# Two transformer blocks: an FFN's down projection over 512 tokens, and a PLE stage in a written order

## The chip, the cores and the metric

The kernel runs on one core of one Trainium2 chip. A core has TensorE (PE, matrix products), VectorE (DVE), ScalarE (ACT), GpSimd (POOL) and SyncE (SP), which issues the transfers. The metric is the device time of one execution in microseconds, as a median over runs. A profile of one execution gives the trace.

## The reference, cut to what matters

A first block of two layers gives h, 512 tokens by 1024 features. The second block has two layers, and each ends with these lines (`rms_norm(h, g)` is h / sqrt(mean(h²) + eps) · g, the mean over a token's features):

```python
h = h + rms_norm(mix, post_mix_g[i])
f = conv_ffn(rms_norm(h, pre_ffn_g[i]), w_up[i], conv_w[i], conv_b[i], w_down[i])   # (silu(g) * up) @ w_down
h = h + rms_norm(f, post_ffn_g[i])
gate = jax.nn.sigmoid(rms_norm(h, ple_norm_g[i]) @ w_ple_gate[i])
h = h + gate * (p[i] @ w_ple_proj[i])
```

`conv_ffn` has 2816 hidden features, its down projection goes from 2816 to 1024. The last two lines are the PLE: a projection of p (256 features) to 1024, times a gate of 1024 by 1024. Behind layer 0's PLE comes layer 1's mixer, which begins with `rms_norm(h, pre_mix_g)`; layer 1's PLE writes the output.

## The kernel before

Activations lie with features on the 128 partitions and tokens along the free dimension: h is 128 x 8 x 512. Every product is computed as three products of split float32 numbers. A weight tile w of 128 x 1024 is loaded by SP (`wload`, line 235), ScalarE rounds it to `whi` (L246) and another engine subtracts to get `wlo` (L249, `wsplit`). `lomode` says which: VectorE ("V"), or POOL and VectorE in turn ("VP", in the PLE's gate). Operands are split in the same way. `mm3_steps` then issues for each of the feature blocks three matmuls into one PSUM bank (L279).

The down projection stands at the end of `ffn_main`. `HALVES` are tokens 0 to 255 and 256 to 511. For each half and each of 8 blocks of output features, 22 hidden blocks are multiplied, with weights in three loads; all weights are loaded and split once for each half. `post_evac` copies a block to `fg` with the gain and adds its squares to `acc`. When half 0 is done, `post_add` turns its squares to a factor: TensorE sums over partitions with `mean1k` (`rsc`, L312), VectorE adds eps and POOL takes the power (`rcol`, L315 and L316), TensorE spreads the result over 128 partitions (`rsb`, L320). VectorE multiplies `fg` by it (L1108), POOL and VectorE in turn add it to h (L1109). `scaled_in` makes the gate's operand: ScalarE's copy (L1066) and VectorE's subtraction (L1067), `paA` for half 0 and `paB` for half 1. Half 0's steps run beside the matmuls of half 1.

The `ple` function does the same for half 1, then `scale` sums the squares of h for each half (L1073 ScalarE, L458 VectorE, L461 POOL) and gives `rr`, the norm's factor, which is applied after the product. 48 matmuls of 512 columns give the projection `pp` (L1665). The gate goes by `project8`: half 0 with all 8 weight blocks, then half 1 with the same weights, loaded and split again. For each block `gate` does four steps (L1670 to L1673). In layer 0 the next mixer's norm follows for each half (`norm_in`); the mixer loads its small constants and multiplies `ws` by a triangle mask `tri` (L1261).

An instruction's place in its engine's queue is set by a scheduler with its own model of durations, except inside `manual_schedule` for the engines it names: there they stand as the code issues them. Each engine runs its queue in order. Slots (`_Slots`) interleave generators of instructions: a main stream, whose items each carry a length in nanoseconds, and side streams, of which each takes one step for every call of the slot.

```python
# the slot: one step of every side stream, then the main stream for ns nanoseconds
self.sides = [x for x in self.sides if next(x, self) is not self]
self.debt += ns
```

## Time and profile before

| what | value |
|---|---|
| median of 3 runs | 2337.01 us (2332.03 to 2339.45) |
| the profiled execution | 2340.36 us, its span 2338.6 us |
| TensorE, VectorE, ScalarE, POOL busy | 2244.5, 1707.5, 1140.5, 510.6 us |
| layer 0: down projection from 1419.7, PLE from 1547.0 to 1613.5 us | 127.3 and 66.5 us |
| layer 1: down projection from 2142.1, PLE from 2269.3 to 2334.0 us | 127.2 and 64.7 us |
| mean granted clock of TensorE | 0.983 |

An engine's busy time is the sum of its instructions; the span is the time from the first instruction to the last. PE and PEld are TensorE's matmuls and its weight loads, which run beside each other. A granted clock of 1.00 is TensorE's upper level of 2.4 GHz, 0.50 the lower of 1.2 GHz. In the chain of waits a piece such as "x570" is a run of that many instructions without a gap, so its length divided by the count is the spacing from one start to the next.

### The profile page before, as it was taken

The numbers are of one execution on the slowest core, as the hardware profiler recorded it, in microseconds if no ns is written. First come the engines' busy times: TensorE is split into PE (matmuls) and PEld (weight loads), VectorE is DVE, ScalarE is ACT, GpSimd is POOL, SyncE is SP. The second block draws the span as 40 slices with busy tenths as digits, with TensorE's granted clock in tenths as the row PEclk, the third lists the DMA queues.
The fourth block names the chain that finished last, engine by engine and source line by source line (L and its number), as shares of the span: only waits on it lengthen the run. The fifth ranks groups of instructions, "written<-read, shape, count | busy, mean of one in ns | idle before, by whom it ended". The sixth has DMA issues, their size and how long they took to land.

```text
span 2338.6 us, 37220 instructions
## 1 busy us (share of the span) xinstructions
PE 2244.5 (96%) x14372; PEld 1948.9 (83%) x14372; DVE 1707.5 (73%) x2922; ACT 1140.5 (49%) x2105; POOL 510.6 (22%) x548
## 2 busy tenths in 40 slices
PE   7999999999999998998999999999998999999998
PEld 5877778888888897766898889988876798888998
DVE  5898656746888868877787665669878688666558
ACT  3534443643434344456664444555455665444444
POOL 0110010322444425113121110124204021110004
PEclk9999999999999998999999999999998999999999
DMA  7452124442122244420253335665430153334664
GB/s 287 127 162 92 37 86 148 145 125 90 56 64 64 75 147 148 162 64 28 78 175 99 99 97 148 178 185 178 144 116 19 54 164 118 99 99 116 174 189 136
DMA packets 83746, 279.03 MB, mean 119 GB/s; under 512 B 9584, under 2 KB 14704, under 8 KB 83568
## 3 DMA queue, kind: packets, MB, share of 16 engines
q1 hardware_dynamic: 83568, 276.64, 37.9%
q8 instruction: 113, 1.85, 0.3%
q14 instruction: 65, 0.53, 0.1%
HBM read 274.51 MB, written 2.10 MB: 118 GB/s over the span
## 4 chain that ended last, share of the span: by engine, by line
PE 76%; DVE 15%; ACT 3%; issue 3%; DMA 2%; POOL 2%; SPq 0%; DVEq 0%; ACTq 0%; POOLq 0%
PE mm L279 29%; PE bg L279 23%; PE s L279 4%; DVE wlo L249 3%; PE o L580 2%; PE s L924 2%; PE pt L571 2%; PE bg L845 2%; DMA w<-in_w_ada 2%; PE s L1564 1%; PE pt L279 1%; PE s L845 1%; PE bg L1665 1%; ACT whi L246 1%; PE mm L1377 1%
## 5 line engine op out<-in xcount | busy, mean ns | idle before, releaser
L246 ACT CAST whi<-w 128x1024 fp32r<-128x1024 f32 (+1 forms) x436 | 449.0, 1032 | 568.9 <-PE mm L279 250.2
L249 DVE TENSOR_TENSOR wlo<-w,whi 128x1024 fp32r<-128x1024 f32 (+1 forms) x420 | 524.0, 1250 | 225.1 <-ACT whi L246 222.8
L279 PE MATMUL bg<-a,whi 128*128 128x512 f32 x1280 | 395.7, 391 | 0.0
L279 PEld LDWEIGHTS bg<-a,whi 128*128 128x128 f32 x1280 | 240.4, 188 | 51.2 <-issue 1.0
L279 PE MATMUL mm<-hx,whi 128*128 128x512 f32 x864 | 276.7, 400 | 3.4 <-DVE sga L682 3.1
L279 PE MATMUL mm<-fh,whi 128*128 128x256 f32 x1408 | 252.7, 282 | 0.0
L279 PE MATMUL bg<-a,wlo 128*128 128x512 f32 x640 | 249.7, 391 | 2.6 <-DVE wlo L249 2.6
L279 PEld LDWEIGHTS mm<-fh,whi 128*128 128x128 f32 x1408 | 217.3, 189 | 0.2
L279 PE MATMUL mm<-fh,wlo 128*128 128x256 f32 x704 | 198.9, 284 | 0.6 <-DVE wlo L249 0.6
L279 PEld LDWEIGHTS mm<-hx,whi 128*128 128x128 f32 x864 | 158.4, 190 | 33.3 <-DVE sga L682 3.3
L279 PE MATMUL mm<-a,whi 128*128 128x256 f32 (+1 forms) x768 | 169.4, 316 | 2.4 <-DVE a L254 1.1
L279 PE MATMUL mm<-hx,wlo 128*128 128x512 f32 x432 | 170.1, 394 | 0.0
L1617 POOL TENSOR_TENSOR cv<-cv 128x512 f32<-128x512 f32 x44 | 61.6, 1400 | 386.1 <-DVE cv L1604 386.1
L279 PEld LDWEIGHTS bg<-a,wlo 128*128 128x128 f32 x640 | 120.6, 188 | 29.0 <-DVE wlo L249 4.0
L1604 DVE SCALAR_TENSOR_TENSOR cv<-q,cols,cv 128x511 f32<-128x511 f32 (+1 forms) x176 | 134.4, 766 | 2.5
L279 PEld LDWEIGHTS mm<-fh,wlo 128*128 128x128 f32 x704 | 132.5, 189 | 1.0 <-DVE wlo L249 1.0
L279 PEld LDWEIGHTS mm<-a,whi 128*128 128x128 f32 x768 | 124.8, 196 | 8.8 <-issue 2.3
L1611 DVE TENSOR_TENSOR q<-bg,rr 128x512 f32<-128x512 f32 x74 | 51.1, 691 | 107.6 <-PE bg L279 107.6
L279 PE MATMUL s<-a,whi 128*128 128x256 f32 (+1 forms) x576 | 116.4, 300 | 1.6 <-DVE a L254 1.6
L279 PE MATMUL mm<-a,wlo 128*128 128x256 f32 (+1 forms) x384 | 117.8, 307 | 0.0
L279 PE MATMUL mm<-hc,whi 128*128 128x256 f32 x576 | 110.0, 289 | 2.3 <-ACT k L813 2.2
L279 PEld LDWEIGHTS s<-a,whi 128*128 128x128 f32 x576 | 92.9, 194 | 5.6 <-DVE a L254 1.9
(461 smaller groups left out, 4948.9 us busy)
## 6 DMA issues: line engine op xcount, KB each, us to landing
w<-in_wup SPq DMA_DIRECT2D x102, 512.0 KB, 3.6
w<-in_wdn SPq DMA_DIRECT2D x64, 448.0 KB, 3.4
w<-in_w_ada SPq DMA_DIRECT2D x48, 512.0 KB, 3.6
w<-in_w_c SPq DMA_DIRECT2D x48, 512.0 KB, 3.5
w<-in_w_in SPq DMA_DIRECT2D x38, 512.0 KB, 4.5
w<-in_wo SPq DMA_DIRECT2D x32, 512.0 KB, 3.5
w<-in_wdn SPq DMA_DIRECT2D x32, 512.0 KB, 3.6
w<-in_wpg SPq DMA_DIRECT2D x32, 512.0 KB, 3.8
```

The costliest lines, as they stand in the source:

```text
L246: self.nc.scalar.copy(hi[:, :c], w)
L249: eng.tensor_sub(lo[:, :c], w, hi[:, :c])
L279: self.nc.tensor.matmul(ps, w[a][:, (k - k0) * c:(k - k0 + 1) * c], x[b](k), start=first and n == 0, stop=last and n == 3 * len(ks) - 1)
L571: nc.tensor.transpose(pt[:, c:c + 128], P[g][:, i, kb * 128:(kb + 1) * 128], self.ident)
L580: self.nc.tensor.matmul(o[64 * g:64 * g + 64, 2 * rp:2 * rp + 2, :].rearrange("p a b -> p (a b)"), vt[:, keys[kb], 64 * g:64 * g + 64], pb ...
L845: nc.tensor.matmul(p, xf(k, a, t), w[b][:, 512 * k2:512 * k2 + 512], start=k == 0 and i == 0, stop=k == 7 and i == 2)
L924: nc.tensor.matmul(s_[:, c, :], lhs(c), rhs(c), start=True, stop=True)
L1377: nc.tensor.matmul(p, self.a[a][:, k, 128 * t:128 * t + 128], w[b][:, 512 * k2:512 * k2 + 512], start=k == 0 and i == 0, stop=k == 7 and i ...
L1564: nc.tensor.matmul(s_[:, j, :], qst[:, 2 * (2 * rp + i) + g, q0:q0 + 128], kst[b][x][:, g, :W], start=j == x == 0, stop=False, skip_group_ ...
L1604: nc.vector.scalar_tensor_tensor(t[:, s:], p[:, :S - s], cw(i), t[:, s:], op0=ALU.mult, op1=ALU.add)
L1611: nc.vector.tensor_mul(q, p, self.rr)
L1617: nc.gpsimd.tensor_mul(a, a, b)
```

## The change

The down projection takes all 512 tokens at once, 8 blocks of 528 matmuls in all, with one pass over the weights. `post_add` and `scaled_in` for the halves are gone from the loop.

The PLE is written out as generators. `projected` issues the projections, `gates` the gate. As a side stream `added` takes a step for every slot: after two projections it issues the norm of f for 512 tokens, then VectorE's chain in a fixed order (L1681, L1682, L1687, eight rounds, half 0 first), then, behind the chain's last instruction, three weight splits and the square sums for `rr`. `gates` first takes half 0 of blocks 0 to 2, then half 1 of these, whose weights are kept (`kw`, or `whi` and `wlo` for block 0). Their evictions come together behind them. In layer 0 blocks 3 to 7 follow half by half from weights split once, with the next mixer's norm of half 0 as a side stream; in layer 1 they go at full width. POOL keeps only the power in the PLE. VectorE takes h's add, all splits, the fold of the squares (L461) and the mixer's `ws` times `tri` (L1269, which was L1261).

```diff
-                sq = tmp.tile([128, sl.stop - sl.start], F32, name="psq", tag="psq", bufs=2)
+                n = sl.stop - sl.start
+                sq = tmp.tile([128, n], F32, name="psq", tag="psq" if n < S else "nq", bufs=2 if n < S else 4)
...
-        nc.gpsimd.tensor_mul(ws, ws, tri[:, None, :].to_broadcast([128, 8, 128]))
+        nc.vector.tensor_mul(ws, ws, tri[:, None, :].to_broadcast([128, 8, 128]))
...
-        wd = d[f"wdn{l}"]
-        for sl in HALVES:
-            for m in range(8):
-                p = self.bk("mm", [128, 256])
-                for c0, c1 in ((0, 8), (8, 15), (15, 22)):
-                    w = self.wsplit(wd[m, :, 128 * c0:128 * c1])
-                    self.mm3(p, w, [lambda k, t=t: t[:, k, sl] for t in fh], c0, c1 - c0, c0 == 0, c1 == NF)
-                evac(m, sl, p)
-                if sl is HALVES[1] and m == 0:
-                    self.scaled_in("ple_norm", l, HALVES[0], pa)
-            if sl is HALVES[0]:
-                self.post_add(self.nrm, fg, acc, sl)
-                pa = self.ap.tile([128, 2, 8, 256], F32R, name="paA", tag="a1", bufs=1)
         pl = [[None] * 2, [None] * 2]
...
+        wd = d[f"wdn{l}"]
+        cuts = ((0, 8), (8, 15), (15, 22))
+        wq = self.wqueue([wd[m, :, 128 * a:128 * b] for m in range(8) for a, b in cuts])
+        with self.tc.manual_schedule(engines={mybir.EngineType.PE}):
+            for m in range(8):
+                p = self.bk("mm", [128, S])
+                for a, b in cuts:
+                    self.mm3(p, next(wq), [lambda k, t=t: t[:, k, :] for t in fh], a, b - a, a == 0, b == NF)
+                evac(m, slice(0, S), p)
+        return fg, acc, pl
...
-        pb = fp.tile([128, 2, 8, 256], F32R, name="paB")
-        self.post_add(self.nrm, fg, acc, HALVES[1])
+        if l == 0:
+            pa = [self.ap.tile([128, 2, 8, 256], F32R, name="paA", tag="a1", bufs=1), fp.tile([128, 2, 8, 256], F32R, name="paB")]
+            part = lambda j, hf: pa[hf][:, j, :, :]
+        else:
+            pa = [self.ap.tile([128, 8, S], F32R, name="paA", tag="a1", bufs=1), fp.tile([128, 8, S], F32R, name="paB")]
+            part = lambda j, hf: pa[j][:, :, HALVES[hf]]
         rr = fp.tile([128, S], F32, name="rrp")
-        self.scaled_in("ple_norm", l, HALVES[1], pb)
-        for sl in HALVES:
-            self.scale(rr[:, sl], sl)
-        w = [self.wsplit(d[f"wpp{l}"][k]) for k in range(2)]
-        for m in range(8):
-            p = self.big()
-            for i, (k, a, b) in enumerate([(k, a, b) for k in range(2) for a, b in ((0, 0), (0, 1), (1, 0))]):
-                nc.tensor.matmul(p, w[k][a][:, 128 * m:128 * m + 128], pl[b][k], start=i == 0, stop=i == 5)
-            self.evict(pp[:, m, :], p)
+        wp = [self.wsplit(d[f"wpp{l}"][k]) for k in range(2)]
+        wg = d[f"wpg{l}"]
+        keep = lambda: [fp.tile([128, 1024], F32R, name="kw", tag="kw", bufs=10) for _ in range(2)]
+        ws = {0: self.wsplit(wg[0])}
+        ws.update((m, self.wsplit(wg[m], *keep())) for m in (1, 2))
+        def added():
+            for _ in range(2):
+                yield
+            pr = yield from self.rstd_steps([acc], S, self.mean1k, NORM_EPS, self.nrm)
+            with self.tc.manual_schedule(engines={mybir.EngineType.DVE}):
+                for hf, sl in enumerate(HALVES):
+                    for i in range(4):
+                        v, h = fg[:, 2 * i:2 * i + 2, sl], self.h[:, 2 * i:2 * i + 2, sl]
+                        nc.vector.tensor_mul(v, v, pr[:, None, sl].to_broadcast([128, 2, 256]))
+                        nc.vector.tensor_add(h, h, v)
+                        for k in (2 * i, 2 * i + 1):
+                            x, g = self.h[:, k, sl], self.c("ple_norm", 8 * l + k)
+                            hi, lo = (part(j, hf)[:, k, :] for j in range(2))
+                            nc.scalar.activation(hi, x, AF.Copy, scale=g)
+                            end = nc.vector.scalar_tensor_tensor(lo, x, g, hi, op0=ALU.mult, op1=ALU.subtract)
+            with self.tc.issue_after(end.ins):
+                for m in (3, 4, 5):
+                    ws[m] = self.wsplit(wg[m], *keep())
+                for n, sl in enumerate(HALVES):
+                    sq = self.sumsq(lambda i, t: nc.scalar.activation(t, self.h[:, 2 * i:2 * i + 2, sl], AF.Square), 256, self.nrm,
+                                    fold=nc.vector)
+                    for _ in range(1 if n else 13):
+                        yield
+                    nc.scalar.copy(rr[:, sl], (yield from self.rstd_steps(sq, 256, self.mean1k, NORM_EPS, self.nrm)))
+            self.tap(f"hf{l}", self.h)
+        def projected():
+            for m in range(8):
+                p = self.bk(("mm", "s", "pt")[m % 3], [128, S])
+                for i, (k, a, b) in enumerate([(k, a, b) for k in range(2) for a, b in ((0, 0), (0, 1), (1, 0))]):
+                    nc.tensor.matmul(p, wp[k][a][:, 128 * m:128 * m + 128], pl[b][k], start=i == 0, stop=i == 5)
+                nc.scalar.copy(pp[:, m, :], p)
+                yield 1361
 
         def gate(m, sl, p):
-            t = self.nrm.tile([128, 256], F32, name="gp", tag="gp", bufs=2)
+            t = fp.tile([128, S], F32, name="gt", tag="gt", bufs=2)[:, :sl.stop - sl.start]
...
-        self.lomode = "VP"
-        self.project8(d[f"wpg{l}"], lambda j, k, sl: (pa if sl is HALVES[0] else pb)[:, j, k, :], HALVES, gate, after)
-        self.lomode = "V"
+        def half(p, w, hf):
+            return self.mm3_steps(p, w, [lambda k, j=j: part(j, hf)[:, k, :] for j in range(2)])
+        def gates():
+            first = range(3)
+            ps = [self.bk(b, [128, S]) for b in ("mm", "mm", "s")]
+            late = []
+            for hf, sl in enumerate(HALVES):
+                for m in first:
+                    yield from half(ps[m][:, sl], ws[m], hf)
+                    if hf:
+                        late.append(lambda m=m: gate(m, slice(0, S), ps[m]))
+                        if m == 2:
+                            for x in late:
+                                x()
+            ws.update((m, self.wsplit(wg[m])) for m in (6, 7))
+            if l:
+                for m in range(3, 8):
+                    p = self.bk(("mm", "s", "s")[m % 3], [128, S])
+                    yield from self.mm3_steps(p, ws[m], [lambda k, x=x: x[:, k, :] for x in pa])
+                    gate(m, slice(0, S), p)
+                return
+            for hf, sl in enumerate(HALVES):
+                for m in range(3, 8):
+                    p = self.bk(("mm", "s", "s")[m % 3], [128, 256])
+                    yield from half(p, ws[m], hf)
+                    gate(m, sl, p)
+                if hf == 0:
...
+                    slot.side(self.norm_in_steps(self.nrm, "pre_mix", 1, sl))
+        slot = _Slots(all_of(projected(), gates()))
+        with self.tc.manual_schedule(engines={mybir.EngineType.PE}):
+            slot.side(added())
+            while True:
+                slot(1400)
+                if slot.debt == 0.0:
+                    break
+            assert not slot.sides
+        if l == 0:
+            self.norm_in(self.nrm, "pre_mix", 1, HALVES[1])
```

The order of the engines' instructions shows what becomes of it. First VectorE in layer 0's PLE before, from the norm's `rcol` of half 1 to the gate (`nq` are squares, `gp` the gate's work tile, `pp` the projection).

```order
L1108 TENSOR_TENSOR ffg<-ffg,rsb 128x2x256 x4
L267 COPY pp<-bg 128x512
L1109 TENSOR_TENSOR h<-h,ffg 128x2x256
L249 TENSOR_TENSOR wlo<-w,whi 128x1024
L1109 TENSOR_TENSOR h<-h,ffg 128x2x256
L315 TENSOR_SCALAR rcol<-rsc 128x2
L1067 SCALAR_TENSOR_TENSOR paB<-h,cols,paB 128x256 x4
L458 TENSOR_TENSOR nq<-nq 128x512
L1067 SCALAR_TENSOR_TENSOR paB<-h,cols,paB 128x256 x4
L458 TENSOR_TENSOR nq<-nq 128x512 x2
L249 TENSOR_TENSOR wlo<-w,whi 128x1024 x2
L1670 TENSOR_TENSOR gp<-bg,rrp 128x256 x2
```

The same place now, from the fourth round of half 1 (the chain's last) on; `gt` is the gate's work tile.

```order
L1681 TENSOR_TENSOR ffg<-ffg,rsb 128x2x256
L1682 TENSOR_TENSOR h<-h,ffg 128x2x256
L1687 SCALAR_TENSOR_TENSOR paB<-h,cols,paB 128x256 x2
L249 TENSOR_TENSOR kw<-w,kw 128x1024
L458 TENSOR_TENSOR nq<-nq 128x512
L249 TENSOR_TENSOR kw<-w,kw 128x1024 x2
L458 TENSOR_TENSOR nq<-nq 128x512 x3
L461 TENSOR_TENSOR nq<-nq 128x256
L458 TENSOR_TENSOR nq<-nq 128x512 x2
L315 TENSOR_SCALAR rcol<-rsc 128x2
L461 TENSOR_TENSOR nq<-nq 128x256
L249 TENSOR_TENSOR wlo<-w,whi 128x1024
```

The sums of squares and the fold (L461) now stand on VectorE behind the whole chain and three kept-weight splits; before they were among half 1's subtractions, with POOL doing the fold. `rcol` (L315) stands behind the fold.

Next TensorE. Before, in layer 0's PLE, the square sum's `rsc` for half 0 stood early in half 0's gate matmuls:

```order
L279 MATMUL bg<-paA,wlo 128x256
L279 MATMUL bg<-paA,whi 128x256 x2
L279 MATMUL bg<-paA,wlo 128x256
L279 MATMUL bg<-paA,whi 128x256 x4
L312 MATMUL rsc<-mean1k,nq 128x1 x2
L279 MATMUL bg<-paA,wlo 128x256
L279 MATMUL bg<-paA,whi 128x256 x2
L279 MATMUL bg<-paA,wlo 128x256
```

And now, in half 1 of blocks 0 and 1 (`whi` and `wlo` are block 0's weights, `kw` block 1's):

```order
L279 MATMUL mm<-paB,whi 128x256 x2
L279 MATMUL mm<-paB,wlo 128x256
L312 MATMUL rsc<-mean1k,nq 128x1 x2
L279 MATMUL mm<-paB,whi 128x256 x2
L279 MATMUL mm<-paB,wlo 128x256
L279 MATMUL mm<-paB,whi 128x256 x2
L279 MATMUL mm<-paB,wlo 128x256
L279 MATMUL mm<-paB,whi 128x256 x2
L279 MATMUL mm<-paB,wlo 128x256
L320 MATMUL rsb<-ident,rcol 128x128 x2
L279 MATMUL mm<-paB,kw 128x256 x12
L312 MATMUL rsc<-mean1k,nq 128x1 x2
```

`rsc` moved from the first gate block of half 0 to the middle of half 1 of block 0, with the rest of half 1 of blocks 0 to 2 behind it.

Last POOL between layer 0's down projection and the next mixer, before:

```order
L316 TENSOR_TENSOR rcol<-rcol,mhalf 128x2
L461 TENSOR_TENSOR nq<-nq 128x256
L249 TENSOR_TENSOR wlo<-w,whi 128x1024
L316 TENSOR_TENSOR rcol<-rcol,mhalf 128x2
L249 TENSOR_TENSOR wlo<-w,whi 128x1024 x3
L316 TENSOR_TENSOR rcol<-rcol,mhalf 128x2
L249 TENSOR_TENSOR wlo<-w,whi 128x1024
L254 TENSOR_TENSOR a_15597<-nt,a_15596 128x256 x2
L249 TENSOR_TENSOR wlo<-w,whi 128x1024
L254 TENSOR_TENSOR a_15597<-nt,a_15596 128x256 x2
L1147 MEMSET vcz 128x512
L1261 TENSOR_TENSOR ws<-ws,tri 128x1024
```

And now:

```order
L316 TENSOR_TENSOR rcol<-rcol,mhalf 128x2
L1625 TENSOR_TENSOR cv<-cv 128x512 x22
L316 TENSOR_TENSOR rcol<-rcol,mhalf 128x4
L316 TENSOR_TENSOR rcol<-rcol,mhalf 128x2 x3
L254 TENSOR_TENSOR a_14962<-nt,a_14961 128x256 x4
L1155 MEMSET vcz 128x512
L1281 MEMSET z 128x8 x2
L316 TENSOR_TENSOR rcol<-rcol,mhalf 128x2
```

The adds to h, the fold, the weight splits and `ws` are gone, so a power waits for none of them.

## Rows read from the trace of the kernel before

**Rows 1.** The page: span; busy time, share, instructions of each engine

```profile
span 2338.6 us, 37220 instructions
...
PE 2244.5 (96%) x14372; PEld 1948.9 (83%) x14372; DVE 1707.5 (73%) x2922; ACT 1140.5 (49%) x2105; POOL 510.6 (22%) x548
```

**Rows 2.** Windows: stretch, us, busy PE PEld DVE ACT POOL; PEclk, DMA share, GB/s

```profile
1419.70:1547.00 127.30, 127.00 (x1063) 126.76 (x1063) 72.95 (x85) 64.00 (x94) 7.19 (x5) 1.00 0.63 182
1547.00:1613.50 66.50, 62.27 (x463) 59.64 (x462) 56.04 (x85) 36.53 (x64) 32.98 (x19) 0.97 0.54 165
...
2269.30:2334.00 64.70, 60.97 (x452) 58.32 (x450) 52.86 (x78) 32.00 (x52) 28.96 (x14) 0.97 0.46 141
1575.30:1578.60 3.30, 3.30 (x15) 3.30 (x16) 3.15 (x4) 0.75 (x2) 3.30 (x2) 0.50 0.69 171
...
1636.90:1640.10 3.20, 3.20 (x17) 3.20 (x17) 1.22 (x5) 1.01 (x2) 0.00 (x0) 0.50 0.38 146
1340.00:1400.00 60.00, 60.00 (x266) 49.69 (x265) 40.39 (x51) 26.28 (x34) 6.47 (x5) 1.00 0.31 96
```

**Rows 3.** The chain of waits, 1409 to 1670: start, us, what, count

```profile
1419.90 68.40 PE mm L279 x570
...
1497.85 1.14 DVE wlo L249
...
1499.30 2.06 DVE paA L1067 x5
...
1503.02 44.18 PE mm L279 x370
1547.20 6.84 PE bg L1665 x30
...
1631.78 2.36 POOL ws L1261
1634.15 1.65 POOL rcol L316
```

**Rows 4.** Waits of PE, 1547 to 1667: us in total, times, longest

```profile
PE rsb L320 <- POOL rcol L316: 3.2, 1, 3.2
PE bg L279 <- DVE wlo L249: 2.8, 1, 2.8
PE bg L279 <- POOL wlo L249: 0.9, 1, 0.9
PE mm L845 <- DVE wlo L249: 0.8, 1, 0.8
PE mm L845 <- DVE gp L1670: 0.5, 1, 0.5
```

**Rows 5.** Lines by form, 1419 to 1670: count | busy, mean ns | idle

```profile
L249 DVE TENSOR_TENSOR wlo<-w,whi 128x1024 fp32r<-128x1024 f32 x40 | 52.6, 1319 | 23.7 <-ACT whi L246 23.6
...
L249 DVE TENSOR_TENSOR wlo<-w,whi 128x896 fp32r<-128x896 f32 x31 | 34.6, 1118 | 31.0 <-ACT whi L246 30.9
...
L249 POOL TENSOR_TENSOR wlo<-w,whi 128x1024 fp32r<-128x1024 f32 x8 | 21.9, 2740 | 11.1 <-ACT whi L246 11.1
...
L1067 DVE SCALAR_TENSOR_TENSOR paB<-h,cols,paB 128x256 fp32r<-128x256 f32 x8 | 5.4, 732 | 0.0
...
L1108 DVE TENSOR_TENSOR ffg<-ffg,rsb 128x512 f32<-128x512 f32 x8 | 5.0, 682 | 2.5 <-PE rsb L320 2.5
...
L1066 ACT ACTIVATE paA<-h,cols 128x256 fp32r<-128x256 f32 x8 | 3.5, 497 | 0.0
L1067 DVE SCALAR_TENSOR_TENSOR paA<-h,cols,paA 128x256 fp32r<-128x256 f32 x8 | 3.3, 473 | 0.0
```

**Rows 6.** The chain of waits, 2315 to 2339, the kernel's end

```profile
2314.99 19.00 PE bg L279 x160
...
2334.01 0.43 DVE gp L1670
...
2335.37 0.42 DVE h L1673
```

More of the change, by code (lines that the diff above doesn't have):

```diff
@@ L1046, in c_out, with norm_in, norm_in_steps @@
             self.norm_out(nrm, "pre_mix", 0, sl, sq, bank)
-    def norm_in(self, tmp, gain, l, sl, dst=None):
+    def norm_in(self, *args):
+        now(self.norm_in_steps(*args))
+    def norm_in_steps(self, tmp, gain, l, sl):
         nc = self.nc
@@ L1053, in norm_in @@
         sq = self.sumsq(lambda i, t: nc.scalar.activation(t, self.h[:, 2 * i:2 * i + 2, sl], AF.Square), n, tmp)
-        self.norm_out(tmp, gain, l, sl, sq, dst=dst)
+        for _ in range(4):
+            yield
+        pr = yield from self.rstd_steps(sq, n, self.mean1k, NORM_EPS, tmp)
+        self.normed(tmp, pr, lambda k: self.h[:, k, sl], lambda k: self.c(gain, 8 * l + k), range(8), sl)
     def norm_out(self, tmp, gain, l, sl, sq, bank="o", dst=None):
@@ L1058, in norm_out, with scaled_in @@
         self.normed(tmp, pr, lambda k: self.h[:, k, sl], lambda k: self.c(gain, 8 * l + k), range(8), sl, dst)
-    def scaled_in(self, gain, l, sl, dst=None):
+    def scaled_in(self, gain, l, sl, dst=None, ks=range(8)):
         nc = self.nc
-        for k in range(8):
+        for k in ks:
             hi, lo = (x[:, k, sl] for x in self.a) if dst is None else (dst[:, j, k, :] for j in range(2))
@@ L1066, in scaled_in @@
             nc.scalar.activation(hi, x, AF.Copy, scale=g)
-            nc.vector.scalar_tensor_tensor(lo, x, g, hi, op0=ALU.mult, op1=ALU.subtract)
+            last = nc.vector.scalar_tensor_tensor(lo, x, g, hi, op0=ALU.mult, op1=ALU.subtract)
+        return last
     def scale(self, rr, sl):
@@ L1675, in gate, with all_of @@
                 nc.sync.dma_start(self.out[m, :, sl], self.h[:, m, sl])
-        def after(pi, sl):
-            if l == 0:
-                if pi == 0:
-                    self.new_a()
-                self.norm_in(self.nrm, "pre_mix", 1, sl)
-        self.lomode = "VP"
-        self.project8(d[f"wpg{l}"], lambda j, k, sl: (pa if sl is HALVES[0] else pb)[:, j, k, :], HALVES, gate, after)
-        self.lomode = "V"
+        def half(p, w, hf):
[25 more added lines that the diff above has]
+                if hf == 0:
+                    self.new_a()
+                    slot.side(self.norm_in_steps(self.nrm, "pre_mix", 1, sl))
+        def all_of(*its):
+            for x in its:
+                yield from x
+        slot = _Slots(all_of(projected(), gates()))
[8 more added lines that the diff above has]
+            self.norm_in(self.nrm, "pre_mix", 1, HALVES[1])
         self.tap(f"he{l}", self.h)
```

5 lines of the change are left out of this document (2 added, 3 removed).

## Prediction

> **What bounds the kernel now.** I read the page first: TensorE is busy 2244.5 of 2338.6 us (96%), VectorE 73% [rows 1], so time goes when TensorE runs fewer cycles or waits less. Next the windows, cut where layer 0 of the second block changes stage [rows 2]: the down projection fills 127.30 us with 127.00 busy at clock 1.00, so there the cost is the number of matmuls times their spacing; the PLE stage behind it holds 62.27 busy in 66.50 us (layer 1: 60.97 in 64.70), with pieces at granted clock 0.50, the 1.2 GHz level. The chain of waits [rows 3] then gives the spacing, and the list of waits [rows 4] what TensorE stood for: VectorE's and POOL's low weight parts (2.8 and 0.9 us; layer 1's list has the same two rows), a second wait at the next mixer's norm, `rsb` for POOL's `rcol` (3.2), and two short ones (0.8, 0.5). Last I took VectorE's durations from the lines by form [rows 5], since the new PLE is a VectorE chain.
>
> **Down projection.** 1056 matmuls of 256 columns become 528 of 512. Spacing of 256 columns: 68.40/570 = 0.120, 44.18/370 = 0.1194 [rows 3]. Of 512: 60.00/266 = 0.2256 in the up projection [rows 2], 6.84/30 = 0.228 in the PLE projections [rows 3]. So 528 × 0.227 = 119.9 against 127.3: −7.4 per layer, −14.8 in all (−13.8 to −16.4 by the two spacings). The weights' splits halve and stay hidden: 24 on VectorE at 1.1 to 1.3 us [rows 5] in 120 us, where 48 fitted. SP issues 24 weight loads fewer here and 8 fewer in each PLE; at a DMA share of 0.54 to 0.63 [rows 2] nothing waited for them, so I cost that at nothing.
>
> A rule speaks against this size. The Trainium skill (TensorE: Matmul & The Clock Gate, "Back-to-back issue gap") gives an isolated matmul its columns over 2.4 GHz plus 2.5 ns; two halves would cost only 2.5 ns more than one full matmul. By it, estimated, both layers save 1056 × 2.5 ns = 2.6 us, not 14.8. The trace disagrees: twice 0.1197 is 0.239 against 0.227.
>
> **PLE, layer 0.** Let T be the first projection matmul (1547.2 before). Before, TensorE began half 0 of the gate at once with the projections' end, because half 0 of h was normed beside the down loop. Now the whole 512 tokens' norm, add and scaling start at T. Following the new order:
> 1. The eviction, square and sum of the last down block take some 3 us (two ScalarE steps and a VectorE add at about 0.6 to 0.7 for 512 columns, behind a weight split). `rsc` stands behind two projections (12 × 0.227 = 2.7), `rsb` behind a third; with `rcol`'s add and power VectorE could start at T+5.2. Two kept-weight splits of 1.14 [rows 3] are in its queue there; one still runs: T+6.1.
> 2. Eight pairs of [multiply, add, two subtractions, with ScalarE's copy between]: 0.68 + 0.68 + 0.50 + 2 × 0.47 [rows 5], less what back-to-back instructions overlap (five subtractions in 2.06 are 0.41 each [rows 3]), plus hand-offs of 0.02 to 0.03: 2.7 each, 21.6 together. Inside stand two weight splits (1.14) and the mask multiply of `ws`, partly in the gaps while ScalarE copies: +3.5.
> 3. TensorE: 48 projections end at T+10.9. Half 0 of block 0 is paced by the chain until T+6.1+10.8+2.3 = T+19.3 (8 us idle where before had work). The remaining 49 matmuls of half 0 run at 0.119 (19.00/160 [rows 6]) to T+25, and 15 of half 1 are paced to T+28.6.
> 4. There stands `rsc` for the first half's square sum. Its fold is the eighth instruction behind the chain's end on VectorE: three kept-weight splits (3.4), three sums for half 0 and one for half 1 (0.6 to 0.68 each), the fold (0.4). Ready at T+6.1+21.6+3.5+6.2 = T+37.4; I take 37, since some sums begin early. TensorE waits 8.4 us, and behind that `rsc`, in TensorE's order, are 57 ready matmuls (6.8 us): the nine of block 0, block 1's, block 2's. This wait replaces both weight waits.
> 5. From T+37: `rcol` and power, 0.9 of wait, 57 × 0.119 = 6.8, small matmuls 0.6, then the clock: after the 2.8 us wait for `wlo` [rows 4] the row at 1575.30 has 15 matmuls in 3.30 us at clock 0.50, where 1.8 would do [rows 2]: 1.5 lost. Then 240 × 0.119 = 28.6 and about 0.6 of norm matmuls: T+76.0, against 66.5 before: **+9.5**.
>
> Cover and cost: without POOL's part VectorE has no partner in these stretches. Before, POOL took h adds and every second weight split at 2.74 us [rows 5], and VectorE's `paB` subtractions beside them mean 0.732 against 0.473 for `paA`. I price the chain undisturbed; with the disturbed rows a pair costs 3.2 and the splits 1.32, +4.0 + 0.9 per layer.
>
> **PLE, layer 1.** Same order, no `ws` multiply: fold at T+36.2, so 0.8 less; the last five blocks full width, 120 × 0.227 = 27.2 for 28.6. Together T+73.2 against 64.7: **+8.5**.
>
> **Next mixer and tail.** The waits on `gp` and `wlo` (1.3) go since less stands on VectorE at the gate's end. `rcol`'s power stood behind POOL's 2.36 us `ws` multiply [rows 3], itself late for `tri`; with the multiply moved to VectorE the 3.2 us wait falls to about 1 and the slow clock behind it (17 matmuls in 3.20 us at 0.50 [rows 2], 1.2 lost) goes: −1.3 − 2.2 − 1.2 = −4.7. But SP now issues the mixer's constants (`wg` among them) after the next weights, and VectorE's split of `wg` stands ahead of the norm's last `rcol`: if `wg` comes later than now by one 512 KB load (3.2 us at the 165 GB/s of the stage [rows 2]), wait and slow clock stay and grow, and with −1.3 the place costs +2. I take −3.5, between −5.7 (no wait left) and +2. Tail: four steps from 2334.01 to 2335.79 (1.78 [rows 6]) become 512 wide, four at about 0.66: +0.9, and the last output transfer is twice as big: +0.5 (0 to 1; what follows the last step now is 2338.6 − 2335.79 = 2.8). **+1.4**.
>
> **Sum.** −14.8 + 9.5 + 8.5 − 3.5 + 1.4 = +1.1, to the profiled execution's 2340.36 (1.8 around its span of 2338.6): 2341.5. That execution lies 3.35 above the median of 2337.01, so on the median's scale 2338.1. I forecast **2338: no measurable change**. A difference under 0.3% (7 us) can't be told from none.
>
> **Rivals.**
> - *The chain is quicker.* With instructions at their back-to-back starts (0.60, 0.60, 0.50, 0.41, 0.41) a pair is 2.5, and splits that fall wholly into ScalarE's gaps save 2: 3.6 less per layer, and the clock need not fall as long (−0.7). 2 × 4.3, with −1.5 at the mixer: 2338 − 10 = 2328. For: five subtractions in 2.06 us. Against: each pair's ScalarE copy is a real hand-off. Chance 0.24.
> - *Slower: the clock stays down.* The stall of 8 us is longer than any seen here (3.2). If TensorE stays at 1.2 GHz for all 57 second-half matmuls instead of 15, 42 more at about 0.1 lost each: 4.2 per layer, 2338 + 8.4 = 2346. It decides from some 35 more slow matmuls per layer on. Against: both slow pieces of before ended after 15 to 17. Chance 0.13.
> - *Slower: VectorE stays disturbed.* If what stretched `paB` was not POOL but ScalarE's or the DMA's traffic, 4.9 per layer: 2338 + 9.8 = 2348. Chance 0.1.
> - *Slower: the wide matmul saves nothing.* If 0.120 came from this stage's operands and weights and not from the width, a 512-column matmul here costs twice as much and the down term is 0: 2338 + 14.8 = 2353. Against: 256 columns cost the same 0.119 in the gate [rows 6], 512 the same 0.226 to 0.228 in two stages. Chance 0.04. By the Trainium skill's gap rule cited above, the estimate is 2338 + 12.2 = 2350.
>
> **How the numbers follow.** The forecast holds 0.49, itself 2331 to 2345 (mixer −2 to +6, spacing ±1.3, chain ±1.5 per layer). Faster: the first rival, mostly, and the lower edge: 0.25. Slower: the three others, and the late `wg`: 0.28. Same: 0.47. For 8 in 10 the range takes in the first rival's better half and the slower ones: 2326 to 2349.
>
> **What would show it.** Down projection near 120 us at 0.227 a matmul, clock 1.00. In each PLE a wait of TensorE for VectorE's fold (line 461) of 7 to 10 us, 28 to 29 us after the first projection, followed by some 15 slow matmuls; VectorE's 512-column steps at 0.68. The forecast fails if that wait is under 4 or over 13 us, or if the next `rsb` wait stays above 3. A faster change than forecast must show the fold before T+33.

## The result, and the profile after

The changed kernel takes 2349.39 us (median of 4 runs, 2347.74 to 2351.49), the kernel before 2334.97 in the same comparison (4 runs). The ratio is 1.0063, 95% interval 1.0045 to 1.0081: slower by 14.4 us, where no measurable change was forecast (2338). The profiled execution took 2351.49 us, its span 2347.5.

First the page of the changed kernel, the lines that answer to [rows 1].

```profile
span 2347.5 us, 34331 instructions
...
PE 2241.6 (95%) x13196; PEld 1891.6 (81%) x13196; DVE 1626.6 (69%) x2834; ACT 1077.7 (46%) x2003; POOL 436.0 (19%) x516
```

Every engine does less, TensorE by 1176 matmuls, and the span is longer: the time went into waits and into stretches at the lower clock. The windows show in which stage; they answer to [rows 2], with the same columns (stretch, us, busy PE, PEld, DVE, ACT, POOL, granted clock, DMA share, GB/s).

```profile
1418.70:1541.90 123.20, 123.20 (x530) 99.11 (x529) 35.37 (x36) 33.55 (x43) 1.30 (x1) 1.00 0.35 104
1541.90:1620.00 78.10, 66.30 (x468) 62.70 (x467) 58.02 (x105) 39.18 (x72) 6.01 (x8) 0.91 0.23 72
2142.90:2266.10 123.20, 123.20 (x529) 99.12 (x528) 35.38 (x36) 33.53 (x43) 1.29 (x1) 1.00 0.35 104
2266.10:2341.20 75.10, 64.34 (x337) 55.49 (x335) 46.31 (x73) 29.51 (x51) 2.57 (x3) 0.91 0.16 53
1579.50:1585.20 5.70, 5.70 (x27) 5.70 (x28) 2.83 (x5) 1.49 (x3) 0.87 (x1) 0.50 0.15 60
```

The down projection fell from 127.3 to 123.2 us in each layer, with TensorE busy all the time at clock 1.00. The PLE grew from 66.5 to 78.1 and from 64.7 to 75.1. Its busy time hardly grew (62.27 to 66.30 in layer 0), its idle time did, from 4.2 to 11.8 us. The last row is a piece at the lower clock level, behind the fold. There is an earlier one, in the first half of the gate, which VectorE's chain paces: TensorE was busy 2.42 of 5 us, and then ran at 0.50 (same columns).

```profile
1556.00:1561.00 5.00, 2.42 (x13) 1.67 (x12) 4.96 (x9) 3.40 (x7) 0.00 (x0) 1.00 0.31 105
1561.50:1564.50 3.00, 3.00 (x16) 3.00 (x16) 2.42 (x4) 0.91 (x2) 0.00 (x0) 0.50 0.30 79
```

What TensorE waited for, layer 0 from 1541 and then layer 1 from 2140 (total, times, longest):

```profile
PE rsc L312 <- DVE nq L461: 9.2, 1, 9.2
PE mm L279 <- ACT paA L1686: 1.6, 2, 1.4
PE rsb L320 <- POOL rcol L316: 1.5, 1, 1.5
...
PE rsc L312 <- DVE nq L461: 8.6, 1, 8.6
```

One wait for VectorE's fold stands out in each layer, and the weight waits of [rows 4] are gone. The chain of waits shows the spacing of the down projection, and what led to the fold (start, us, what, count):

```profile
1409.88 8.84 PE bg L279 x39
1418.72 123.19 PE mm L279 x528
1541.92 1.37 PE mm L1704 x6
...
1568.02 0.70 DVE h L1682
...
1570.80 0.70 DVE h L1682
...
1574.01 0.69 DVE nq L458
1574.69 2.27 DVE kw L249 x2
...
1578.32 0.69 DVE nq L458
...
1579.49 0.98 PE rsc L312 x4
1580.48 2.13 PE mm L279 x9
1582.61 0.43 PE rsb L320 x2
1583.03 2.43 PE mm L279 x12
1585.46 0.34 PE rsc L312 x4
...
1587.34 0.22 PE rsb L320 x2
```

123.19 / 528 = 0.2333 us a matmul, against 8.84 / 39 = 0.2267 in the up projection just before it, with the same width and the same weight tiles. Behind VectorE's last add to h (1570.80) come sums (`nq`) and kept-weight splits (`kw`, 2.27 for the last two of three) before `rsc` may start at 1579.49, 37.6 us after the first projection.

### The profile page after: what moved, and what is told of

Read it like the earlier page. It is cut to its first block, busy times and chain, and to the rows that moved or that the text cites. A ratio compares the mean times of both kernels' runs of the same rounds, so it can differ in the third digit from the quotient of the medians.

```text
span 2347.5 us, 34331 instructions
## 1 busy us (share of the span) xinstructions
PE 2241.6 (95%) x13196; PEld 1891.6 (81%) x13196; DVE 1626.6 (69%) x2834; ACT 1077.7 (46%) x2003; POOL 436.0 (19%) x516
## 4 chain that ended last, share of the span: by engine, by line
PE 77%; DVE 14%; ACT 3%; issue 2%; DMA 1%; POOL 1%; SPq 0%; DVEq 0%; ACTq 0%; POOLq 0%
PE mm L279 30%; PE bg L279 21%; PE s L279 6%; DVE wlo L249 2%; PE o L580 2%; PE s L924 2%; PE pt L571 2%; PE bg L845 2%; PE s L1572 1%; DMA w<-in_w_ada 1%; PE pt L279 1%; PE s L845 1%; ACT whi L246 1%; PE mm L1385 1%; PE s L736 1%
## 5 line engine op out<-in xcount | busy, mean ns | idle before, releaser
L249 DVE TENSOR_TENSOR wlo<-w,whi 128x1024 fp32r<-128x1024 f32 x362 | 450.8, 1247 | 298.8 <-ACT whi L246 296.3
L246 ACT CAST whi<-w 128x1024 fp32r<-128x1024 f32 x362 | 375.8, 1040 | 607.3 <-PE mm L279 317.1
L279 PE MATMUL mm<-fh,whi 128*128 128x512 f32 x704 | 221.1, 395 | 0.0
L279 PEld LDWEIGHTS mm<-fh,whi 128*128 128x128 f32 x704 | 132.1, 188 | 32.0
L279 PE MATMUL mm<-fh,wlo 128*128 128x512 f32 x352 | 139.0, 395 | 0.0
L316 POOL TENSOR_TENSOR rcol<-rcol,mhalf 128x2 f32<-128x2 f32 (+1 forms) x31 | 25.0, 805 | 490.7 <-DVE rcol L315 490.7
```

Source lines behind the costliest of these rows:

```text
L246: self.nc.scalar.copy(hi[:, :c], w)
L249: eng.tensor_sub(lo[:, :c], w, hi[:, :c])
L279: self.nc.tensor.matmul(ps, w[a][:, (k - k0) * c:(k - k0 + 1) * c], x[b](k), start=first and n == 0, stop=last and n == 3 * len(ks) - 1)
L316: nc.gpsimd.tensor_tensor(col, col, self.mhalf[:, :nt], op=ALU.pow)
```

## The experiments

Two questions: why a matmul of the down projection costs 0.2333 and not 0.227, and what the PLE's wait is made of. Each kernel was timed beside the kernel before, whose medians in these comparisons were 2333.5, 2333.6 and 2334.5. Runs of one kernel spread by 4 to 14 us, so two or three microseconds between two rows of the table mean little by themselves. Lengths of stages read in the profiles are steadier and are given beside the medians where they decide. There a PLE stage runs from its first projection matmul to the next mixer's first matmul (layer 0) or to the start of the gate's last matmul (layer 1).

| kernel | median us (runs) | to the kernel before, 95% interval |
|---|---|---|
| changed | 2349.39 (4) | 1.0063, 1.0045 to 1.0081 |
| with a break in the down projection | 2350.95 (4) | 1.0071, 1.0056 to 1.0086 |
| with `fh` moved by 128 bytes | 2343.55 (10) | 1.0033, 1.0018 to 1.0049 |
| with `fh`'s two parts interleaved | 2345.52 (1) | one run, no interval |
| with the old down loop | 2356.87 (4) | 1.0089, 1.0060 to 1.0118 |
| with the fold first | 2342.48 (5) | 1.0034, 1.0021 to 1.0047 |
| with `rsc` behind half 1 | 2335.60 (10) | 1.0009, 0.9996 to 1.0022 |
| with sums in the chain too | 2338.08 (10) | 1.0017, 1.0005 to 1.0029 |
| before, `ws` on VectorE | 2337.30 (10) | 1.0010, 0.9996 to 1.0024 |
| before, once more | 2333.14 (1) | one run, no interval |
| combined | 2316.65 (6) | 0.9921, 0.9909 to 0.9933 |

### A break in the down projection

In the kernel before, small matmuls of the norm stood inside the loop; the change leaves 528 alike in a row. The rival "history" says that the spacing comes from that. Four dummy one-column products (each issued as two matmuls) go ahead of the second block:

```diff
+                if m == 1:
+                    pc = self.bk("o", [128, 4], "rsc")
+                    for t in range(4):
+                        nc.tensor.matmul(pc[:, t:t + 1], self.ident, self.mean1k[:, 0:1], start=True, stop=True)
```

> Changed kernel, plus four one-column matmuls of constants whose result nobody reads, put once per layer in front of the second output block of the down projection. In the changed kernel its 528 matmuls stand 233.3 ns apart, where I had reckoned with 227. Theory 'history': TensorE falls into a rhythm at the start of a run and keeps it until something interrupts the run (in the kernel before, the spacing went from 120.0 to 118.7 at the small sum matmuls in the middle of the down projection, with the same operands). Then the spacing of the seven blocks behind the interruption is 226 to 229, each down projection takes 120.5 to 121.5 instead of 123.2 us, and the kernel is 4 to 5 us faster than the changed one. Theory 'place': operands, width and where they lie set the spacing. Then it is 233.3 behind the interruption too, and the time is that of the changed kernel plus about 0.5 us.

Measured 2350.95, not told apart from the changed kernel. In its chain of waits the spacing ahead of the break is 15.39 / 66 = 0.2332 and behind it 107.47 / 462 = 0.2326:

```profile
1417.24 15.39 PE mm L279 x66
1432.63 0.79 PE rsc L1653 x8
1433.41 107.47 PE mm L279 x462
```

A break is worth 0.6 ns a matmul. "History" falls as the reason for the 6 ns.

### The operand moved by 128 bytes

In the compiled program (a profile shows no addresses) the weight tiles and the up projection's operand begin 224 bytes above a multiple of 256; the two parts of `fh`, the down projection's operand, begin 96 above one. An unused tile of 128 bytes a partition ahead of `fh` puts them on 224 as well. The two parts of `fh` are alone in their pool, and nothing else in the program is changed.

```diff
+        hp.tile([128, 32], F32R, name="shift")
         fh = [hp.tile([128, NF, S], F32R, name=f"fh{i}") for i in range(2)]
```

> Changed kernel, with an unused tile of 128 bytes per partition in front of the two fh tiles, the down projection's moving operand; nothing else differs. In the built program the weight tiles, and the moving tiles of the up projection (227 ns a matmul), begin at 224 above a multiple of 256 bytes, fh at 96; with the shift fh begins at 224 too. Theory 'place': the spacing of 512-column matmuls depends on how the moving operand lies against the weights, so the down projection runs at 226 to 228 ns: 119.5 to 120.5 instead of 123.2 us per layer, 6 to 7 us in all off the changed kernel. Theory 'width or stage': what sets 233 is the length of a bank's run (66 matmuls) or the weights' change three times per bank; then 233 stays and the time is that of the changed kernel.

Measured 2343.55. The chain of waits of this kernel, and the windows of both down projections:

```profile
1421.94 119.47 PE mm L279 x527
```

```profile
1421.80:1541.20 119.40, 119.40 (x528) 98.89 (x527) 35.32 (x36) 33.50 (x42) 1.29 (x1) 1.00 0.34 106
2139.40:2258.90 119.50, 119.50 (x529) 98.93 (x528) 35.31 (x36) 33.55 (x42) 1.29 (x1) 1.00 0.34 106
```

119.47 / 527 = 0.2267, the up projection's spacing, in both layers. The fold's waits stayed at 9.2 and 8.6 us. So the operand's place in memory costs 6.6 ns a matmul, 3.5 us a layer. The two stages give 7.0 us; the medians differ by 5.8. Whether the operand's own place or its place against the weights counts, this run does not tell.

### The two parts interleaved

Rival: it is the distance between `fh`'s high and low part, not the place. Here they lie 2048 bytes apart, on the same offset as in the changed kernel.

```diff
-        fh = [hp.tile([128, NF, S], F32R, name=f"fh{i}") for i in range(2)]
+        both = hp.tile([128, NF, 2, S], F32R, name="fh")
+        fh = [both[:, :, j, :] for j in range(2)]
```

> Changed kernel, with the high and low parts of fh in one tile, block by block beside each other (2048 bytes apart instead of 45056), beginning at the same address as before (96 above a multiple of 256 bytes). Theory 'offset against the weights': the spacing stays near 233, since each block lies as before against the weights modulo 256 bytes. Theory 'distance of the two parts': the spacing falls or rises by more than 2 ns. Theory 'width or stage': 233.3 unchanged.

The chain shows 123.19 us for 528 matmuls again, 0.2333:

```profile
1417.32 123.19 PE mm L279 x528
```

At this offset the distance doesn't matter.

### The old down loop with the new PLE

The down projection goes back to two halves with 48 weight loads (without the norm of half 0 between them); the PLE stays as changed.

```diff
-        wq = self.wqueue([wd[m, :, 128 * a:128 * b] for m in range(8) for a, b in cuts])
...
+        for sl in HALVES:
             for m in range(8):
-                p = self.bk("mm", [128, S])
+                p = self.bk("mm", [128, 256])
                 for a, b in cuts:
-                    self.mm3(p, next(wq), [lambda k, t=t: t[:, k, :] for t in fh], a, b - a, a == 0, b == NF)
-                evac(m, slice(0, S), p)
+                    w = self.wsplit(wd[m, :, 128 * a:128 * b])
+                    self.mm3(p, w, [lambda k, t=t: t[:, k, sl] for t in fh], a, b - a, a == 0, b == NF)
+                evac(m, sl, p)
```

> Changed kernel with the down projection as it was in its loop: two halves of 256 columns, weights loaded and split once for each half, no norm between the halves; the new PLE behind it. It prices the down projection's part of the change alone. By what the traces show (127.3 against 123.2 us per layer) it is 8 us slower than the changed kernel if the rest stays; with my forecast of the term (14.8) it would be 15 us slower. A rival: at 118.7 ns a matmul throughout, the rhythm that the kernel before has in its second half, 126 us, 5 us slower.

Measured 2356.87, 7.5 above the changed kernel. The chain of this kernel:

```profile
1419.65 126.72 PE mm L279 x1056
```

126.72 / 1056 = 0.1200, so the wide matmul saves 2 × 0.1200 − 0.2333 = 6.7 ns a pair, in both layers 7.1 us. A small effect of history shows here too: in the kernel before, 40 us of the second half, behind the norm's matmuls, hold 339 matmuls and 40 us of the first 336; without these matmuls both hold 336. The new PLE is the whole loss: 2356.87 / 2333.59 is 23 us over the kernel before.

### The fold first

VectorE's three sums and the fold of half 0 stand ahead of the kept-weight splits, nothing else moves on TensorE.

```diff
+        class adder:
+            tensor_add = staticmethod(lambda *x: folds.append(nc.vector.tensor_add(*x)))
...
+                sl = HALVES[0]
+                sqs = [self.sumsq(lambda i, t: nc.scalar.activation(t, self.h[:, 2 * i:2 * i + 2, sl], AF.Square), 256, self.nrm,
+                                  fold=adder)]
+                end = folds[0]
...
                 for m in (3, 4, 5):
                     ws[m] = self.wsplit(wg[m], *keep())
```

> Changed kernel, with the first half's sums and their fold put straight behind the chain on VectorE, ahead of the three kept-weight splits; TensorE's order is unchanged. Theory 'order': the wait of 9.2 and 8.6 us is made of what stands on VectorE between the chain's end and the fold, 6.2 us, of which the three splits are 3.4 and one sum of the other half 0.6. Then TensorE's wait for the fold falls to 5 to 6 us in each layer and the kernel is 6 to 8 us faster than the changed one. Theory 'given back': the splits and the other half's sums then come later and TensorE waits for the second factor or for the kept weights instead; the fold's wait falls but a new wait of 2 to 4 us stands behind it, and the gain is under 3 us.

Measured 2342.48, 6.9 us faster than the changed kernel. The wait in layer 0 and in layer 1 (`adder` is at line 1675):

```profile
PE rsc L312 <- DVE nq L1675: 5.3, 1, 5.3
...
PE rsc L312 <- DVE nq L1675: 4.7, 1, 4.7
```

The wait fell by 3.9 in each layer, 7.8 in both. So the place of the fold behind the splits was 3.9 us of the 9.2. The rest is the end of VectorE's chain (it runs on for some 2.7 us after TensorE has come to `rsc`) and half 0's own sums and fold (2.5 us from the last subtraction to the fold's end). The two PLE stages became 6.2 us shorter, of the 6.9.

### `rsc` behind half 1

TensorE does all 72 half-1 matmuls of blocks 0 to 2 ahead of `rsc`; the evictions, which need `rr`, come behind it, and the accumulator banks of blocks 3 to 7 change places. VectorE's splits of the last two weight blocks move behind the chain with it.

```diff
-                    for _ in range(1 if n else 13):
+                    for _ in range(1 if n else 18):
                         yield
...
+            for x in late:
+                x()
...
-                    p = self.bk(("mm", "s", "s")[m % 3], [128, 256])
+                    p = self.bk(("s", "s", "mm", "mm", "s")[m - 3], [128, 256])
```

> Changed kernel, with the first half's sum matmuls put behind all 72 matmuls of half 1 on TensorE instead of behind the first 15, so that 57 ready matmuls (6.8 us) no longer stand behind the wait; evictions of blocks 0 to 2 come behind the factor, and the banks of blocks 3 to 7 are swapped so that block 3 needs none of theirs. VectorE's order behind the chain is nearly unchanged. Theory 'order': the wait for the fold falls by the 6.8 us less what the chain still paces of half 1 (it ends at about T+31.5), to 1 to 3 us, the low clock behind it goes, and the kernel is 12 to 16 us faster than the changed one, 0 to 3 us on either side of the kernel before. Theory 'given back': the evictions come later, TensorE waits for banks or for VectorE in blocks 4 to 7, and the gain is under 8 us.

Measured 2335.60, 13.8 us faster than the changed kernel; the interval holds no change against the kernel before. The waits in layer 0 and in layer 1:

```profile
PE rsc L312 <- DVE nq L461: 4.2, 1, 4.2
...
PE rsc L312 <- DVE nq L461: 2.3, 1, 2.3
```

They fell by 5.0 and 6.3 us, 11.3 in sum: the ready matmuls behind `rsc` were held back for nothing. The PLE stages became 3.7 and 6.5 us shorter, 10.2 of the 13.8; the rest lies outside them. Layer 0 gained less; there the fold itself came later, 40.1 us after the first projection instead of 37.4: weight splits now stand ahead of it on VectorE, the last of them late for its transfer. Behind the wait the clock was at 0.50 again for some 6 us. The chain of waits and the window (columns as before):

```profile
1581.18 1.23 DVE wlo L249
...
1583.01 0.35 DVE nq L461
```

```profile
1583.50:1589.60 6.10, 6.10 (x28) 6.10 (x29) 1.60 (x4) 0.54 (x2) 0.87 (x1) 0.50 0.28 93
```

The expectation had VectorE's order behind the chain nearly unchanged; it was not.

### Sums in the chain too

Both edits, and the square sums of half 0 inside the rounds of half 1.

```diff
+                        if hf:
+                            next(sq0)
+                            if i == 3:
+                                for _ in squares(1):
+                                    pass
+                    sq0 = squares(0)
```

> Both moves: the first half's sums stand inside the second half's rounds of the chain, the second half's sums straight behind it, the kept-weight splits last on VectorE, and the sum matmuls behind all of half 1 on TensorE. Theory 'order': no wait for the fold is left (it is ready at about T+32, TensorE comes at T+38), the stage of layer 0 takes 66 to 68 us and that of layer 1 63 to 65, and the kernel is 17 to 21 us faster than the changed one, 3 to 6 us faster than the kernel before. Theory 'given back': the splits come 3 us later and blocks 3 to 5 wait for their kept weights, 2 to 4 us per layer; the kernel then is no faster than with the late sum matmuls alone.

Measured 2338.08, 11.3 faster than the changed kernel, short of what was expected and no better than the experiment before. The fold's wait is gone, but the waits moved (layer 0, then layer 1):

```profile
PE rsb L320 <- POOL rcol L316: 2.0, 2, 1.8
PE mm L279 <- ACT paB L1703: 2.0, 1, 2.0
...
PE mm L279 <- ACT paA L1703: 3.6, 3, 2.0
```

TensorE now waits for ScalarE's copies of the operands. The sums lengthen each round of half 1 on VectorE from 2.8 to 3.4 us; ScalarE stands idle until VectorE's add to h is done, and makes its last pair of copies in layer 0 30.1 us after the first projection instead of 28.3. In the profiles the two PLE stages together are 3.0 us shorter than in the experiment before (71.0 and 69.0 against 74.6 and 68.5), but the mixer between them took 524.4 us instead of 519.7, with the same code in both. Why the mixer's time differs so from run to run was not found.

### Before, with `ws` on VectorE

The one part of the change that was to help the next mixer, done alone in the kernel before.

```diff
-        nc.gpsimd.tensor_mul(ws, ws, tri[:, None, :].to_broadcast([128, 8, 128]))
+        nc.vector.tensor_mul(ws, ws, tri[:, None, :].to_broadcast([128, 8, 128]))
```

> Kernel before, with one line of the change: the mixer's product of ws and the mask on VectorE instead of POOL. It prices that part alone. The stage from the gate's end to the first compress matmul is 5.2 us shorter in the changed kernel than before. Theory 'ws': the product on POOL, late for its mask, held up the norm's power, and moving it takes away the 3.2 us wait and the low clock behind it: 3 to 5 us faster than the kernel before. Theory 'the rest of the PLE': what shortened that stage is that VectorE and POOL no longer carry gate work and weight splits into it; then moving ws alone gives under 1.5 us, since VectorE has 1.2 us more to do in the same place and waits for the mask itself.

Measured 2337.30: no gain. Its waits around the mixer's start:

```profile
PE rsb L320 <- POOL rcol L316: 1.5, 1, 1.5
```

The `rsb` wait fell to 1.5, and a wait of 0.6 for a weight split came up.

### Before, once more

> The kernel before once more, for a second profile: its first profile (span 2338.6 us) is slower than its median (2333.5 of 19 to 20 runs). From the end of layer 0's gate (first L845 matmul) to the start of layer 1's down projection it took 528.5 us there, 519.7 to 523.0 in the profiles of the changed kernel and of its variants. Theory 'the change shortens the mixer': the second profile shows 527 to 530 for that stretch again. Theory 'one slow profile': it shows 521 to 525, and of the 5 us that I counted as gained in the next mixer little is left. The down projections are 127.2 to 127.4 and the PLE stages 66.5 and 64.7 us again by either.

2333.14 us, span 2331.4. Its `rsb` wait:

```profile
PE rsb L320 <- POOL rcol L316: 2.2, 1, 2.2
```

It is 2.2, where [rows 4] have 3.2, and its chain reaches the `rsb` without the clock's fall that followed in [rows 2]. The execution that I had priced was the slower one there by some 3 us.

### Combined

`fh` on offset 224 (in layer 1 `paB` and the kept weights too), `rsc` behind half 1, and VectorE's chain in software-pipelined order: a pair's multiply and add come before the pair before's two subtractions, so that ScalarE's copy runs beside them; squares, sums and kept-weight splits stand behind the whole chain. The core of it:

```diff
+                last = None
...
+                            copy = nc.scalar.activation(part(0, hf)[:, k, :], self.h[:, k, sl], AF.Copy, scale=self.c("ple_norm", 8 * l + k))
+                        if last:
+                            lows(*last)
+                        last = hf, i
+                lows(*last)
+                with self.tc.issue_after(copy.ins):
+                    for hf in range(2):
+                        for _ in squares(hf):
+                            pass
+                end = folds[1]
```

> All that the runs before pointed to, in one kernel: fh shifted by 128 bytes (and, in layer 1, paB and the kept weights); sum matmuls behind half 1 on TensorE; on VectorE the multiply and add of the next pair stand ahead of the subtractions of the last, so that VectorE need not stand while ScalarE copies; squares, sums and kept-weight splits all behind the chain on ScalarE and VectorE. By the measured rows a pair then costs VectorE 0.60 + 0.60 + 2 x 0.41 = 2.0 instead of 2.7 us, the chain's first half ends at about T+16 (layer 0) and its second at T+24, TensorE has half 1 of blocks 0 to 2 done at T+30 and waits for no fold. Theory 'order and place': PLE stages of 60 to 64 and 58 to 62 us, down projections of 119.7, and 20 to 30 us off the changed kernel, 2318 to 2328 us, faster than both. Theory 'given back': ScalarE, which carries the projections' evictions, the copies and the squares, becomes the pace of the chain, or the evictions of the first blocks hold up the banks; then the stages stay above 66 us and the time is 2328 to 2336.

Measured 2316.65: 32.7 us under the changed kernel's median, and faster than the kernel before by 0.8% (0.7 to 0.9). The four stages:

```profile
1419.50:1539.20 119.70, 119.70 (x530) 99.13 (x529) 35.32 (x36) 33.55 (x42) 1.29 (x1) 1.00 0.34 107
1539.20:1605.20 66.00, 62.65 (x467) 58.69 (x467) 56.91 (x104) 38.82 (x72) 7.16 (x8) 1.00 0.25 85
2127.00:2246.60 119.60, 119.60 (x529) 99.06 (x528) 35.33 (x36) 33.48 (x42) 1.29 (x1) 1.00 0.34 106
2246.60:2308.30 61.70, 59.49 (x337) 50.87 (x335) 45.60 (x73) 29.39 (x51) 3.31 (x3) 1.00 0.18 65
```

Against the changed kernel that is −3.5, −12.1, −3.6 and −13.4, in sum −32.6. Waits of layer 0's PLE:

```profile
PE rsb L320 <- POOL rcol L316: 1.4, 1, 1.4
PE s L279 <- DVE kw L249: 1.0, 1, 1.0
```

None is longer than 1.4 us, and the granted clock stays at 1.00 through both PLEs. Layer 0's 66.0 us lies a little above the 60 to 64 expected of it, and the whole came out 1.4 us under the lowest time expected (2318). The new order of VectorE's chain was not run alone: the two PLE stages became 25.5 us shorter, and how much of that is the new order's is not known.

## Why the prediction was wrong, point by point

**Down projection: the step "528 × 0.227" failed.** It took the spacing of 512 columns from the up projection and the PLE's projections as that of this stage. Measured is 0.2333, so a layer saved 4.1 us instead of 7.4, 8.2 in all instead of 14.8: 6.6 us missed, the largest part. The working's own sign for this stage, "near 120 us at 0.227 a matmul", did not come. The runs show what the rows did not: with the operand shifted by 128 bytes the term comes out as forecast (119.47 us). The rival "the wide matmul saves nothing" named the right kind of reason, this stage's operands, at a chance of 0.04; its size, no saving, was too much.

The Trainium skill's rule (TensorE: Matmul & The Clock Gate, "Back-to-back issue gap") gave 2350 and the kernel took 2349.39; that they meet is chance. Two halves cost 6.7 ns more than one full matmul with the operand as it lies, not its 2.5, so the down projections saved 8.2 us and not 2.6, and the PLE lost 4.0 more than the working had. Halves of a shifted operand were not timed.

**PLE: the wait was where the working put it, the sum a little short.** Expected were a wait for the fold of 7 to 10 us, 28 to 29 us after the first projection. Measured: 9.2 and 8.6 us; in layer 0 TensorE reached `rsc` 28.4 us after it and went on at 37.6 (I had 37). The stages grew by 11.6 and 10.4, in sum 22.0, against 9.5 + 8.5 = 18.0. Of the 2.1 missed in layer 0, 0.6 lie before the fold's end. From there to the last of the 57 matmuls the working had 9.8 us (0.9 of wait, 6.8, 0.6 for small matmuls, 1.5 for the clock). Measured are 10.9 (1579.49 to 1590.43): the wait did not come, but the four groups of small matmuls took 1.97 (0.98 + 0.43 + 0.34 + 0.22, the first two at 0.50), and the clock, at 0.50 for 5.70 us with 21 gate matmuls where I had counted 15, cost 2.1. The last 0.4 lie in the 240 matmuls behind. In layer 1 the fold came 0.3 later than worked out, the piece behind it took 11.0 for 9.8, and the full-width blocks cost 0.2290 and 0.2333 to 0.2342 instead of 0.227, 0.5 us for the 120; together that is the 1.9 missed there, to within 0.1. The low clock from 1561 on, which the working did not have, cost nothing, since TensorE then had to stand for the fold.

"Kept-weight splits ahead of the fold" and "ready matmuls behind `rsc`" were both named in the working, as 3.4 and 6.8 us a layer. Taken away alone they gave 6.9 and 13.8 us on the medians. That these are just twice the prices is in part chance: the PLE stages became shorter by 2.9 and 3.3 us in the one, by 3.7 and 6.5 in the other.

**The other rivals.** The chain was not quicker: the fold was late, not early. VectorE was not disturbed: `paB` subtractions take 483 ns here, against 732 in [rows 5]. The clock's rival was right in sign: 21 slow matmuls behind the fold instead of 15, not 57.

**Next mixer and tail.** From layer 0's last gate matmul to layer 1's down projection the changed kernel takes 522.95 us, the kernel before 525.24 in its second profile: −2.3 against −3.5. Other variants of the new PLE lie between 519.7 and 524.4 here, so I can't tell −2.3 from −3.5. The late `wg` that the working feared is there (a 5.69 us transfer ends right ahead of the norm's `rcol`), and the wait stayed at 1.5 all the same. That `ws` on POOL was the cause isn't borne out: moved alone it gave nothing, and part of the 3.2 us was that execution. From the last matmul's start to the span's end the changed kernel takes 6.36 us (2341.14 to 2347.5), the kernel before 4.91 (2333.69 to 2338.6): 1.45 more, forecast 1.4.

**Sum.** −8.2 + 22.0 − 2.3 + 1.45 = +13.0, measured +14.4 on the medians, where +1.1 was worked out. The misses (6.6, 4.0, 1.2) all point the same way, so none hid another. The rest is within what executions differ by: the down projection begins between 1415.8 and 1422 us in these profiles. Two slips in the working change nothing: 6.1 + 10.8 + 2.3 is 19.2, not 19.3, and 60.00/266 counts matmuls cut by the window's edges (the spacing there is 0.2267).

Not settled: why the offset matters (only two were tried with 512 columns, and the weights were not moved alone), and how much of the mixer's gain is the change's.

## What to carry to other kernels

A spacing read in one stage is a safe price for another only if its operands lie alike: compare their offsets as well as their widths, and where a long stage is paced by TensorE, a shift of the operand is a cheap trial. In an in-order queue, what counts is what stands ready behind a waiting instruction: one `rsc` of four tiny matmuls held back 57 ready ones, and moving it, with the evictions that hang on it, made the two stages 10.2 us shorter (13.8 us on the medians, about as much as the whole change had lost). When a step that ran beside the matmuls of another half becomes a chain at a stage's start, price the chain with all that shares its engine's queue, and put splits and sums behind it.

## What the hardware showed that I had not expected

- A 512-column matmul of split float32 takes 0.2267 us from start to start where operand and weights begin on the same offset (224 modulo 256 bytes), and 0.2333 where the operand lies 128 bytes off. Three stages show the first (up projection; shifted down projection; the combined kernel's wide gate blocks). The wide gate blocks of the changed kernel, where only some operands agree, take 0.2290 with the kept weights and 0.2333 to 0.2342 with the others; no simple count of agreeing operands gives that. The operand is the same in both, so the weights' tiles count too; that agreement of the offsets is the rule is not shown. The chain of the changed kernel's layer 1 and then that of the combined kernel:

```profile
2313.84 5.50 PE mm L279 x24
2319.34 10.99 PE s L279 x48
2330.33 5.60 PE mm L279 x24
2335.93 5.62 PE s L279 x24
```

```profile
2292.10 10.88 PE mm L279 x48
2302.98 5.45 PE s L279 x24
```

- The distance between the operand's two parts (2048 bytes or whole tiles) changed nothing, and a break of eight tiny matmuls under 1 ns a matmul.
- During a wait of 9.2 us the granted clock fell to 0.50 and stayed there for 5.70 us of matmuls behind it; after one of 2.8 us in the kernel before it was so for 3.30 us [rows 2, 4]. A single long wait isn't needed: in the changed kernel it was 0.50 from 1561.5 to 1564.5 too, where no wait ahead of it was over 1.4 us but TensorE had been busy only 2.42 of 5 us. In the combined kernel, with no wait over 1.6 us in the PLE stages, it stayed at 1.00 there.
